# A hybrid trunk on one core: the tokens' rms as a scheduler stream of its own, and new VectorE prices in the scheduler

## Chip, cores and metric

The kernel runs on one core of a Trainium2 chip. The metric is the device time of one execution in microseconds (us). The profile comes from one execution of the same program.

## What is computed

Two layers on 528 tokens (16 meta tokens and 512 inputs) of width 1024, in float32. Cut to what matters here, one layer is:

```python
n = rms_norm(h, mix_norm_g)
q, k, v, qi, ki, wi, xr, yg, cv, gt = split(n @ w_in)
qi, ki = rotary(qi), rotary(ki)                 # indexer: 8 heads of 64
logits = einsum("bqhd,bsd->bqhs", qi, ki)
iscore = einsum("bqhs,bqh->bqs", relu(logits), wi * idx_scale)
sel = top_k(where(admissible, iscore, -inf), 128)   # 128 keys per query
attn = softmax attention of q over the chosen keys and values
rnn = gated linear recurrence of conv4(xr), times gelu(yg)
cnv = silu(layer_norm(conv31(glu(cv))))
merged = g_attn * (attn @ w_o_attn) + g_rnn * (rnn @ w_o_rnn) + g_conv * (cnv @ w_o_conv)
h = h + merged @ w_out
h = h + swiglu(rms_norm(h, ffn_norm_g))
```

## The kernel before

Activations are held with the channels on the partitions, in 8 tiles of 128 x 528. A float32 product is made of float32r parts: each weight tile of 128 x 1024 is loaded by SP's queue into a `raw` buffer, ScalarE copies its high part (`w<-raw`), and the low part is made either by ScalarE (negated copy) with an accumulating transfer on GpSimd's queue (`add_dma`, L401) or by VectorE. `gemm` then multiplies high weights with high and low inputs (L569) and low weights with high inputs (L579). PSUM is four pairs of banks.

Nothing in the program fixes an order by hand. Each job is a generator, a **stream**, that yields its operations one at a time; `Sched.run` simulates five engine clocks with prices and issues, step by step, the operation that can start first (among those within 40 ns of it on the same engine, the one of the best priority). The prices are the cost given with each operation, `LAT` (from the end of an operation to a reader on another engine) and `SELF` (to a reader on the same engine). They decide the order of the instructions on each engine; on the chip each engine then works through its own list in that order, and an instruction that waits holds up all behind it on that engine.

The streams that matter here:

- `main` (priority 40) runs the projection's tiles one after another: the keys of the indexer (`ki`), four tiles of its queries (`qi`), then `v_gemm`, which makes the values and the indexer's weights `wi` (L892), then K tiles, Conformer tiles, and so on. Its epilogues are streams of priority 10.
- The input's norm factor `r` (one number per token, spread over partitions) is made by `rsqrt2`: a sum on TensorE (L652), a root and a square on ScalarE, two operations on VectorE (L383). `r` scales the indexer's queries and keys.
- At the head of `v_gemm`, 4 small matmuls (L866) turn `r` so that tokens lie on the partitions, and VectorE writes `rtok` from them (L387). `v_epi` needs `rtok` to make `wi`. The matmuls on `r` write a half of a bank pair (`pr`), which is free again only when VectorE has read it; `v_gemm` goes on in halves like it, five at a time, and it is part of `main`, so its own matmuls are issued only after that read.
- `choose(i)` for i = 0 to 3 (priorities 36 to 39): 8 steps of scores (L954 or L963 on TensorE, relu on ScalarE, a multiply-add L383 on VectorE), then 16 rounds of `max` (L1004) and `match_replace` (L1005) on VectorE, over 144, 272, 400 and 528 keys. The masks are wanted by `heads` (L1235 on VectorE reads them).
- `k_epi` (rotation L380, then `rsqrt2` and a scaling L383), `ca_epi` and `conv` of the Conformer and recurrent branches share VectorE with it; `conv` is of the lowest priority.

Of the kernel before, what the change touches and what calls it, by code (L numbers as in the profile page):

```python
# [10 lines left out]
FR = mybir.dt.float32r  # L11
AF = mybir.ActivationFunctionType
ALU = mybir.AluOpType

L = 2
T = 528
# [9 lines left out]
TAKEN = -3.4e38  # L26
# [92 lines left out]
          "Abs_reciprocal_sqrt": ("a",)}  # L119
TABLE_LOAD = 1283.0  # L120
MOVE = {"SP": (310.0, 2000.0), "ACTQ": (310.0, 2000.0), "POOL": (210.0, 4300.0)}
SELF = {"PE": 0.0, "DVE": 125.0, "ACT": 110.0, "SP": 0.0, "POOL": 0.0}
LAT = {"PE": 170.0, "DVE": 100.0, "ACT": 130.0, "SP": 0.0, "ACTQ": 0.0, "POOL": 0.0}


class Sched:
    def __init__(self, make):
        self.make = make
        self.slots = {}
        self.clock = {e: 0.0 for e in LAT}  # L130
        self.table = None
# [50 lines left out]
    def spawn(self, gen, prio):  # L182
        self.n += 1
        s = [prio, self.n, gen, None]
        self.streams.append(s)
        self.step(s, None)
# [7 lines left out]
    def start(self, op):  # L194
        t = 0.0
        for b in op.R:
            assert b.live
            r = b.ready + (SELF[b.eng] if b.eng == op.eng else LAT[b.eng] if b.eng else 0.0)
            t = r if r > t else t
        for b in op.W:  # L200
            assert b.live
            if b.eng != op.eng:
                t = max(t, b.ready + (LAT[b.eng] if b.eng else 0.0))
            t = max(t, b.rd)
        return t, max(t, self.clock[op.eng])

    def run(self):
        while self.streams:
# [56 lines left out]
            for b in op.R:  # L265
                b.rd = max(b.rd, done + LAT[e])
            for b in op.W:
# [12 lines left out]
def trunk(ctx, tc, xT, wt, wv, wd, wg, gain_in, par_in, cst_in, id_in, out):  # L280
    nc = tc.nc
    V, S, PE = nc.vector, nc.scalar, nc.tensor

    const = ctx.enter_context(tc.tile_pool(name="const", bufs=1))
# [76 lines left out]
    free, spawn = sch.free, sch.spawn  # L361
# [28 lines left out]
    def dve(cost, fn, R, W):  # L390
        return Op("DVE", cost, fn, R, W)

    def pe(cost, fn, R, W):
        return Op("PE", 1.066 * cost, fn, R, W)
# [13 lines left out]
    def alloc(n=1, dt=FT, keep=0):  # L408
        return Alloc("s", n, dt, keep)
# [363 lines left out]
    def free_pairs(bs):  # L773
        for b in bs:
            free(*b.v)
# [4 lines left out]
    def layer(l, hs, h_src, h_next):  # L780
# [4 lines left out]
        HI, MID, LOW = P_HI, P_MID, P_CONV  # L785
# [68 lines left out]
        wib = boxes(4)  # L854
        rtok = Box()

        def v_gemm(w0, w1):
            vm = const.tile([128, 2, 256], FR, name="vmeta", bufs=1)
            vh = yield alloc(2, FR)
            vl = yield alloc(2, FR)  # L860
            r = yield rbox
            pr = yield Alloc("b1")

            def go():
                for i in range(4):
                    PE.matmul(pr[:, i:i + 1], r[:, NM + 128 * i:NM + 128 * i + 128], ones[:, 1, 0:1], start=True, stop=True)  # L866
            yield pe(900, go, [r], [pr])
            rt_ = const.tile([128, 4], FT, name="rtok", bufs=1)
            yield ts(rt_, pr[:, :4], -0.5 * IDX_SCALE, None, ALU.mult, None, [pr], [])
            free(pr)  # L870
            rtok.set(rt_)
            pss = [None] * 5
            for e, w in enumerate((w0, w1)):
                hi = yield w[0]
                lo = None
                for part in range(2):
                    if part:
                        lo = yield w[1]
                    for i in range(5):
                        t0, tn = (0, 128) if i == 0 else (NM + 128 * (i - 1), 128)  # L880
                        if not e and not part:
                            pss[i] = yield Alloc("b1")
                        ps = pss[i]
                        xk = []
                        for k in range(4 * e, 4 * e + 4):
                            xk.append((yield ns[k]))

                        def go(e=e, part=part, hi=hi, lo=lo, ps=ps, t0=t0, tn=tn, xk=xk):
                            for k, (nh, nl) in enumerate(xk):
                                o = 264 * k  # L890
                                for a, b in (((nh, hi), (nl, hi)), ((nh, lo),))[part]:
                                    PE.matmul(ps[:tn, :264], a[:, t0:t0 + tn], b[:, o:o + 264], start=e + part + k == 0 and a is nh,  # L892
                                              stop=bool(e and part and k == 3))
                        yield pe((920, 460)[part], go, [b for x in xk for b in x] + [(hi, lo)[part]], [ps])
                        if e and part:
                            if i == 0:
                                spawn(v_meta(ps, vm), HI)
                            else:
                                spawn(v_epi(i, tn, ps, vh[(i - 1) // 2], vl[(i - 1) // 2]), HI)
                    free((hi, lo)[part])  # L900
# [70 lines left out]
        def choose(i, box):  # L971
            w, o = W_OF[i], OFF[i]
            q0 = NM + 128 * i
            yield wib[i]
            if i in (0, 1, 3):
                sc = yield Alloc("u" if i == 0 else "s")
                box.set(sc)
            else:
                sc = yield box
            sv = sc[:, o:o + w]  # L980
            for hd in range(8):
                q = yield qi[hd // 2]
                k = yield ki
                t = q[hd % 2]
                ps, v, vw = yield from s_matmul(i, [(t[:, q0:q0 + 128], k[0]), (t[:, q0:q0 + 128], k[1 + hd % 2])], [t, *k], BC)
                rl = yield alloc()
                yield act(vw(rl[:, :w]), v, AF.Relu, [ps], [rl])
                free(ps)
                if hd == 0:
                    yield ts(sv, rl[:, :w], wi[i][:, 0:1], None, ALU.mult, None, [rl], [sc])  # L990
                else:
                    yield stt(sv, rl[:, :w], wi[i][:, hd:hd + 1], sv, ALU.mult, ALU.add, [rl, sc], [sc])
                free(rl)
            idx_left[0] -= 1
            if not idx_left[0]:
                free_pairs(qi)
                free(*ki.v)
                free(rbox.v)
                free(tabs[2].v, tabs[3].v)
            yield dve(80, lambda: V.memset(sv[:64, w - 64:], OUT_OF_REACH), [], [sc])  # L1000
            rows = slice(64, 128) if i == 0 else slice(0, 128)
            for _ in range(16):
                mx = const.tile([128, 8], FT, name=f"mx{i}", bufs=2)
                yield dve(70 + w / 0.96, lambda: V.max(mx[rows], sv[rows]), [sc], [])  # L1004
                yield dve(70 + w / 0.96, lambda: V.match_replace(sv[rows], mx[rows], sv[rows], TAKEN), [sc], [sc])  # L1005
            yield ts(sv[rows], sv[rows], -3e38, -BIG, ALU.is_gt, ALU.mult, [sc], [sc])
            if i == 0:
                yield dve(100, lambda: V.memset(sv[:64, :w - 64], 0.0), [], [sc])
                yield dve(80, lambda: V.memset(sv[:64, w - 64:], -BIG), [], [sc])
            masks[i].set(sc)  # L1010
# [88 lines left out]
        def rnn(c, u, a, m):  # L1099
            yield s4_in  # L1100
            tr = yield rt[0][c]
            sp, sn = s4p[:, l, c:c + 1], s4n[:, l, c:c + 1]
            yield act(a[:, :T], tr[:, :T], AF.Exp, [tr], [a], scale=sn, bias=sn)
            yield act(tr[:, :T], tr[:, :T], AF.Tanh, [tr], [tr], scale=sp, bias=sp)
            yield act(m[:, :T], a[:, :T], AF.Square, [a], [m])
            yield stt(m[:, :T], m[:, :T], 1.0, tr[:, :T], ALU.add, ALU.mult, [m, tr], [m])
            free(tr)
            ti = yield rt[1][c]
            yield stt(u[:, :T], ti[:, :T], 1.0, u[:, :T], ALU.add, ALU.mult, [ti, u], [u])
            free(ti)  # L1110
            yield act(m[:, :T], m[:, :T], AF.Sqrt, [m], [m], scale=0.25)
            yield tt(u[:, :T], u[:, :T], m[:, :T], ALU.mult, [u, m], [u])
            yield dve(620, lambda: V.tensor_tensor_scan(m[:, :T], a[:, :T], u[:, :T], 0.0, ALU.mult, ALU.add), [a, u], [m])
            free(a, u)
            gy = yield rg[c]
            yield tt(m[:, m0:T], m[:, m0:T], gy[:, m0:T], ALU.mult, [m, gy], [m])
            free(gy)
            x, y = yield alloc(2, FR)
            yield from split(x[:, m0:T], y[:, m0:T], m[:, m0:T], [m], x, y)
            free(m)  # L1120
            rs[c].set((x, y))
# [518 lines left out]
        mbox = boxes(4)  # L1640
        for i in range(4):
            spawn(choose(i, mbox[(0, 1, 0, 3)[i]]), P_CHOOSE + i)
        for c0 in range(2):
            spawn(conv(c0), LOW)
        for g in range(2):
# [123 lines left out]
```

## Time and profile before

| | |
|---|---|
| median of 3 executions | 2146.97 us (2145.22 to 2148.07) |
| the profiled execution | 2148.31 us, its span 2146.5 us |
| TensorE (PE) busy | 2093.8 us, 98% |
| its weight loads (PEld) | 1972.3 us, 92% |
| VectorE (DVE) busy | 1591.3 us, 74% |
| ScalarE (ACT) busy | 1361.0 us, 63% |
| GpSimd (POOL) busy | 318.8 us, 15% |
| the chain that ended last | PE 69%, DVE 10%, ACT 3% |

The span is the part of the execution that the profiler saw; the profiled execution is 1.3 us above the median. Busy times add up work of different stages, so a share over the span says little of a single stage: the stages have to be read one by one.

### The profile page before, as it was taken

The page shows a single profiled execution, that of the slowest core. Times are in us where ns is not written, and L with a number is a line of the kernel's source. Part 1 is how long each engine was busy: PE and PEld are TensorE (multiplying, and loading weights), DVE is VectorE, ACT ScalarE, POOL GpSimd, SP SyncE. Part 2 cuts the span into 40 slices and gives each one's busy share as a digit, 9 for nine tenths or more (in the row PEclk, how much of TensorE's full clock was granted, in tenths as well). Part 3 has the DMA queues.
Part 4 walks back from the last instruction along what each step waited for, and adds up shares of the span by engine and source line. Part 5 has one row for each costly group of instructions (what it writes and reads, how often), then busy time and mean ns, then how long its engine had stood idle before and what let it go on. Part 6 is the DMA issues. An engine that isn't in the chain of part 4 may idle for free.

```text
span 2146.5 us, 37980 instructions
## 1 busy us (share of the span) xinstructions
PE 2093.8 (98%) x14808; PEld 1972.3 (92%) x14808; DVE 1591.3 (74%) x2990; ACT 1361.0 (63%) x2114; POOL 318.8 (15%) x392
## 2 busy tenths in 40 slices
PE   7989999999999999999999899999999999999999
PEld 7989989999999999999999898988878888899997
DVE  7899958995337587677669999679962566777774
ACT  7657877876665565455457578888765646555552
POOL 1111101111111011111011121111111211111110
PEclk9999999999999999999999999999999999999999
DMA  8478546788897586657465675567889876766653
GB/s 232 106 171 187 133 91 125 174 179 173 177 214 175 131 194 162 139 138 162 114 195 138 165 181 133 122 135 168 184 181 190 195 180 161 182 153 143 159 137 108
DMA packets 127044, 342.67 MB, mean 160 GB/s; under 512 B 14864, under 2 KB 17040, under 8 KB 126864
## 3 DMA queue, kind: packets, MB, share of 16 engines
q0 software_dynamic: 50112, 145.47, 38.0%
q1 hardware_dynamic: 76608, 194.76, 30.9%
q8 instruction: 116, 1.90, 0.4%
q14 instruction: 64, 0.52, 0.1%
q10 hardware_dynamic: 144, 0.02, 0.0%
HBM read 327.91 MB, written 4.26 MB: 155 GB/s over the span
## 4 chain that ended last, share of the span: by engine, by line
PE 69%; DVE 10%; ACT 3%; issue 2%; DMA 1%; POOL 0%; SPq 0%; DVEq 0%; ACTq 0%; POOLq 0%
PE banks L569 31%; PE banks L579 15%; PE banks L610 12%; PE banks L614 6%; DVE s L383 3%; DVE s L380 3%; ACT s L377 2%; DVE mx L1004 1%; PE banks L1347 1%; DMA s<-in_wt_dram 1%; DVE s L1005 1%; PE banks L954 1%; PE banks L1087 1%; PE banks L1326 1%; DVE u L1005 1%
## 5 line engine op out<-in xcount | busy, mean ns | idle before, releaser
L569 PE MATMUL banks<-s,w 128*128 128x264 f32 (+1 forms) x6432 | 1033.4, 313 | 17.7 <-ACT w L377 7.3
L569 PEld LDWEIGHTS banks<-s,w 128*128 128x128 f32 x6432 | 906.5, 189 | 85.3 <-ACT w L377 7.3
L377 ACT ACTIVATE w<-raw 128x1024 fp32r<-128x1024 f32 (+3 forms) x486 | 479.0, 990 | 286.0 <-PE banks L569 137.5
L579 PE MATMUL banks<-s,w 128*128 128x264 f32 (+1 forms) x3216 | 543.6, 313 | 11.5 <-DMA w<-in_wt_dram 11.5
L579 PEld LDWEIGHTS banks<-s,w 128*128 128x128 f32 x3216 | 461.5, 190 | 47.7 <-DMA w<-in_wt_dram 13.1
L377 ACT ACTIVATE s<-s 128x512 fp32r<-128x512 f32 (+8 forms) x640 | 382.7, 615 | 175.4 <-DVE s L380 137.0
L380 DVE TENSOR_TENSOR s<-s,s 128x528 f32<-128x528 f32 (+8 forms) x522 | 331.0, 654 | 48.6 <-ACT s L377 41.0
L610 PE MATMUL banks<-s,s 128*128 128x264 f32 (+1 forms) x2464 | 347.3, 283 | 5.0 <-DVE s L380 2.5
L401 POOL DMA_DIRECT2D w<-in_wt_dram x192 | 167.3, 871 | 1183.6 <-ACT w L377 1011.7
L383 DVE SCALAR_TENSOR_TENSOR s<-s,half,s 128x512 f32<-128x512 f32 (+23 forms) x480 | 339.8, 743 | 2.8
L610 PEld LDWEIGHTS banks<-s,s 128*128 128x128 f32 x2464 | 318.5, 189 | 7.9 <-ACT s L377 3.1
L380 DVE TENSOR_TENSOR s<-s,banks 128x512 f32<-128x512 f32 (+3 forms) x340 | 195.5, 587 | 110.8 <-PE banks L614 67.6
L377 ACT ACTIVATE s<-banks 128x528 f32<-128x528 f32 (+11 forms) x338 | 165.0, 505 | 155.2 <-PE banks L614 75.4
L614 PE MATMUL banks<-s,s 128*128 128x264 f32 (+1 forms) x1232 | 198.5, 283 | 2.8 <-DMA s<-in_wt_dram 2.8
L401 POOL DMA_DIRECT2D s<-in_wt_dram x132 | 114.1, 864 | 517.8 <-ACT s L377 422.5
L377 ACT ACTIVATE s<-u 128x512 fp32r<-128x512 f32 x176 | 110.4, 627 | 102.3 <-DVE u L380 87.4
L614 PEld LDWEIGHTS banks<-s,s 128*128 128x128 f32 x1232 | 169.5, 189 | 3.2 <-DMA s<-in_wt_dram 3.2
L380 DVE TENSOR_TENSOR s<-u,s 128x512 fp32r<-128x512 f32 x176 | 119.7, 688 | 47.1 <-ACT s L377 42.9
L380 DVE TENSOR_TENSOR w<-raw,w 128x512 fp32r<-128x512 f32 (+2 forms) x94 | 76.1, 814 | 62.7 <-PE banks L569 40.8
L383 DVE SCALAR_TENSOR_TENSOR s<-s,banks 128x528 f32<-128x528 f32 (+1 forms) x48 | 33.2, 692 | 120.0 <-PE banks L579 114.9
L377 ACT ACT_TABLE_LOAD x80 | 102.6, 1283 | 4.9 <-DMA s<-in_xT_dram 3.7
L380 DVE TENSOR_TENSOR u<-s,s 128x512 f32<-128x512 f32 x88 | 60.3, 685 | 25.7 <-DMA s<-in_wt_dram 25.7
(129 smaller groups left out, 1273.5 us busy)
## 6 DMA issues: line engine op xcount, KB each, us to landing
raw<-in_wt_dram SPq DMA_DIRECT2D x206, 512.0 KB, 4.4
w<-in_wt_dram POOLq DMA_DIRECT2D x192, 512.0 KB, 7.7
s<-in_wt_dram SPq DMA_DIRECT2D x176, 256.0 KB, 5.1
s<-in_wt_dram POOLq DMA_DIRECT2D x132, 256.0 KB, 4.8
raw<-in_wd_dram SPq DMA_DIRECT2D x64, 256.0 KB, 2.9
raw<-in_wd_dram SPq DMA_DIRECT2D x16, 384.0 KB, 3.3
s<-s POOLq DMA_DIRECT2D x36, 132.0 KB, 5.6
s<-in_xT_dram SPq DMA_DIRECT2D x16, 264.0 KB, 4.6
```

Source lines behind the costliest of these rows:

```text
L377: return Op("ACT", cost, lambda: S.activation(o, i, f, **kw), R, W, TABLES.get(name))
L380: return Op("DVE", 69 + width(o) / 0.96, lambda: V.tensor_tensor(o, a, b, op), R, W)
L383: return Op("DVE", (69 if isinstance(s, float) else 129) + width(o) / 0.96, lambda: V.scalar_tensor_tensor(o, a, s, b, op0, op1), R, W)
L401: return Op("POOL", 1040.0, lambda: nc.gpsimd.dma_start(out=o, in_=i, accum_op=ALU.add), R, W, None, 4 * o.shape[0] * width(o))
L569: PE.matmul(o, hi[:, 128 * k:128 * k + 128], x, start=(k == ks[0] and i == 0), stop=False)
L579: PE.matmul(o, lo[:, 128 * k:128 * k + 128], x, start=False, stop=k == ks[nk - 1])
L610: PE.matmul(d, w[:, 128 * c:128 * c + 128], t[:, o:o + n], start=c == 0 and e == 0, stop=False)
L614: PE.matmul(d, w[:, 128 * c:128 * c + 128], h[:, o:o + n], start=False, stop=c == 3)
L954: PE.matmul(ps[:, :w], a, b[:, :w], start=e == 0, stop=e == n - 1)
L1004: yield dve(70 + w / 0.96, lambda: V.max(mx[rows], sv[rows]), [sc], [])
L1005: yield dve(70 + w / 0.96, lambda: V.match_replace(sv[rows], mx[rows], sv[rows], TAKEN), [sc], [sc])
L1087: PE.matmul(ps[:, h, :264], w[:, o:o + 128], b[:, 264 * h:264 * h + 264], start=i == 0, stop=i == 2)
```

## The change

Three things are changed, and no arithmetic.

1. `SELF` of VectorE goes from 125 to 15 ns; `LAT` of TensorE from 170 to 200, of VectorE from 100 to 125, of ScalarE from 130 to 140.
2. The prices of `max` and `match_replace` in `choose` go from 70 to 155 and 245 ns, each plus the width over 0.96; that of the scan in the recurrent branch from 620 to 1170 ns.
3. The making of `rtok` leaves `v_gemm` and becomes a stream `tokens`, spawned behind the four `choose` with the priority `HI`, which is 12.

```diff
-SELF = {"PE": 0.0, "DVE": 125.0, "ACT": 110.0, "SP": 0.0, "POOL": 0.0}
-LAT = {"PE": 170.0, "DVE": 100.0, "ACT": 130.0, "SP": 0.0, "ACTQ": 0.0, "POOL": 0.0}
+SELF = {"PE": 0.0, "DVE": 15.0, "ACT": 110.0, "SP": 0.0, "POOL": 0.0}
+LAT = {"PE": 200.0, "DVE": 125.0, "ACT": 140.0, "SP": 0.0, "ACTQ": 0.0, "POOL": 0.0}
...
-        def v_gemm(w0, w1):
-            vm = const.tile([128, 2, 256], FR, name="vmeta", bufs=1)
-            vh = yield alloc(2, FR)
-            vl = yield alloc(2, FR)
+        def tokens():
+
             r = yield rbox
             pr = yield Alloc("b1")
...
             rtok.set(rt_)
+
+        def v_gemm(w0, w1):
+            vm = const.tile([128, 2, 256], FR, name="vmeta", bufs=1)
+            vh = yield alloc(2, FR)
+            vl = yield alloc(2, FR)
...
-                yield dve(70 + w / 0.96, lambda: V.max(mx[rows], sv[rows]), [sc], [])
-                yield dve(70 + w / 0.96, lambda: V.match_replace(sv[rows], mx[rows], sv[rows], TAKEN), [sc], [sc])
+                yield dve(155 + w / 0.96, lambda: V.max(mx[rows], sv[rows]), [sc], [])
+                yield dve(245 + w / 0.96, lambda: V.match_replace(sv[rows], mx[rows], sv[rows], TAKEN), [sc], [sc])
...
-            yield dve(620, lambda: V.tensor_tensor_scan(m[:, :T], a[:, :T], u[:, :T], 0.0, ALU.mult, ALU.add), [a, u], [m])
+            yield dve(1170, lambda: V.tensor_tensor_scan(m[:, :T], a[:, :T], u[:, :T], 0.0, ALU.mult, ALU.add), [a, u], [m])
...
             spawn(choose(i, mbox[(0, 1, 0, 3)[i]]), P_CHOOSE + i)
+        spawn(tokens(), HI)
```

The instructions are the same in number on TensorE, VectorE, GpSimd and SP; ScalarE loads its function table once more. What changes is their order.

TensorE, first layer, from the second `qi` tile to the head of `v_gemm`; `w_236` and `w_303` are the high and low weights of that `qi` tile, `s_300` is `r`. Before:

```order
L569 MATMUL banks<-s_209,w_236 128x264 x2
L569 MATMUL banks<-s_210,w_236 128x264 x2
L579 MATMUL banks<-s_101,w_303 128x264 x2
...
L579 MATMUL banks<-s_209,w_384 128x264 x2
L866 MATMUL banks<-ones,s_300 128x1 x4
L892 MATMUL banks<-w_422,s_380 128x264
```

Now:

```order
L569 MATMUL banks<-s_209,w_236 128x264 x2
L569 MATMUL banks<-s_210,w_236 128x264 x2
L864 MATMUL banks<-ones,s_300 128x1 x4
L579 MATMUL banks<-s_101,w_303 128x264 x2
...
L579 MATMUL banks<-s_209,w_388 128x264 x2
L895 MATMUL banks<-w_424,s_379 128x264
```

The matmuls on `r` moved ahead of the low half of the second `qi` tile and of two whole tiles behind it.

VectorE at the same place; `s_300` is `r`, `s_95` the indexer's keys, `s_379` (now `s_378`) the first normed tile of `v_gemm`. Before:

```order
L383 SCALAR_TENSOR_TENSOR s_301<-banks,s_301 128x528
L337 TENSOR_TENSOR sp_y<-sp_z 128x16
L383 SCALAR_TENSOR_TENSOR s_300<-s_301,s_300 128x528
L338 TENSOR_SCALAR sp_p<-sp_y 128x16
...
L380 TENSOR_TENSOR s_318<-s_318,s_319 128x528
L387 TENSOR_SCALAR rtok<-banks 128x4
L340 SCALAR_TENSOR_TENSOR sp_p<-sp_p,sp_y 128x16
```

Now:

```order
L383 SCALAR_TENSOR_TENSOR s_301<-banks,s_301 128x528
L383 SCALAR_TENSOR_TENSOR s_300<-s_301,s_300 128x528
L383 SCALAR_TENSOR_TENSOR s_378<-s_93,neg,s_300 128x528
L383 SCALAR_TENSOR_TENSOR s_95<-s_95,s_300 128x528
L387 TENSOR_SCALAR rtok<-banks 128x4
L337 TENSOR_TENSOR sp_y<-sp_z 128x16
```

`rtok` moved from behind the rotation of two `qi` tiles to the third place behind `r`.

VectorE in the first layer's choices, around the norm of the first K tile (two L383 of `rsqrt2` that write its factor, a third that scales the tile); `u_784` (now `u_795`) are the scores of `choose(0)`, `s_796` (now `s_817`) those of `choose(1)`. Before:

```order
L1005 MATCH_REPLACE s_796<-mx_1255,s_796 128x272
L1004 MAX mx_1267<-u_784 64x8
L1004 MAX mx_1272<-s_796 128x8
L383 SCALAR_TENSOR_TENSOR s_1181<-banks,s_1181 128x528
L1005 MATCH_REPLACE u_784<-mx_1267,u_784 64x144
L383 SCALAR_TENSOR_TENSOR s_1180<-s_1181,s_1180 128x528
L387 TENSOR_SCALAR u_784<-u_784 64x144
L383 SCALAR_TENSOR_TENSOR s_775<-s_775,s_1180 128x528
```

Now:

```order
L1007 MAX mx_1191<-u_795 64x8
L1007 MAX mx_1184<-s_817 128x8
L383 SCALAR_TENSOR_TENSOR s_1118<-banks,s_1118 128x528
L383 SCALAR_TENSOR_TENSOR s_1117<-s_1118,s_1117 128x528
L383 SCALAR_TENSOR_TENSOR s_770<-s_770,s_1117 128x528
L1008 MATCH_REPLACE u_795<-mx_1191,u_795 64x144
L1007 MAX mx_1227<-u_795 64x8
```

The norm stood in the last round of `choose(0)`, at VectorE's row 184 of the program; it stands in the eighth round from the end now, at row 154, and its three steps follow one another.

## Rows read from the trace of the kernel before

**Rows 1.** The page's busy times: engine, us, share of the span, instructions.
```profile
PE 2093.8 (98%) x14808; PEld 1972.3 (92%) x14808; DVE 1591.3 (74%) x2990; ACT 1361.0 (63%) x2114; POOL 318.8 (15%) x392
```
**Rows 2.** Engine waits, TensorE: what ended them, us in total, times, longest.
```profile
PE banks L579 <- DMA w<-in_wt_dram: 11.5, 5, 3.3
PE banks L892 <- DVE rtok L387: 5.0, 1, 5.0
```
**Rows 3.** Busy us of each engine in chosen stretches, with TensorE's granted clock (PEclk).
```profile
core 0: us, PE busy (x) PEld busy (x) DVE busy (x) ACT busy (x) POOL busy (x), PEclk, DMA share, GB/s
107.30:161.00 53.70, 48.20 (x366) 47.64 (x365) 53.35 (x146) 29.22 (x36) 9.26 (x12) 0.94 0.75 171
28.75:32.16 3.41, 3.41 (x18) 3.41 (x17) 3.37 (x10) 1.99 (x4) 0.00 (x0) 0.50 0.90 197
49.23:56.06 6.83, 5.85 (x26) 5.85 (x27) 6.21 (x16) 2.57 (x4) 0.00 (x0) 0.50 0.47 111
110.67:114.08 3.41, 3.41 (x15) 3.41 (x16) 3.30 (x11) 1.27 (x3) 0.00 (x0) 0.50 0.65 167
137.98:141.39 3.41, 3.41 (x18) 3.41 (x17) 3.41 (x10) 0.14 (x1) 0.47 (x1) 0.50 1.02 240
1192.70:1196.10 3.40, 3.40 (x14) 3.11 (x13) 3.40 (x12) 1.06 (x1) 0.27 (x1) 0.50 1.05 274
```
**Rows 4.** Timeline of TensorE, 25 to 68 us: start, us, instruction, [idle before <-releaser].
```profile
25.73 0.41 PE L569 MATMUL banks<-s,w 128*128 128x264 f32 x2
28.01 3.31 PE L579 MATMUL banks<-s,w 128*128 128x264 f32 x16 [1.87 <-DMA w<-in_wt_dram]
...
43.22 0.95 PE L866 MATMUL banks<-ones,s 128*128 128x1 f32 x8
...
50.21 16.48 PE L892 MATMUL banks<-w,s 128*128 128x264 f32 x112 [4.97 <-DVE rtok L387]
```
**Rows 5.** Timeline of VectorE: `r` is written, and `rtok`.
```profile
29.70 0.71 DVE L383 SCALAR_TENSOR_TENSOR s<-s,s 128x528 f32<-128x528 f32 x1
...
50.00 0.15 DVE L387 TENSOR_SCALAR rtok<-banks 128x4 f32<-128x4 f32 x1
```
**Rows 6.** Timeline of TensorE: waits beside the choices, first layer and second.
```profile
110.66 5.71 PE L569 MATMUL banks<-s,w 128*128 128x264 f32 x32 [3.06 <-DVE s L383]
...
137.17 3.25 PE L579 MATMUL banks<-s,w 128*128 128x264 f32 x16 [2.44 <-DMA w<-in_wt_dram]
...
1146.30 0.52 PE L954 MATMUL banks<-s,s 128*128 128x272 f32 x2 [1.41 <-DVE wi L387]
...
1191.64 3.05 PE L579 MATMUL banks<-s,w 128*128 128x264 f32 x16 [2.66 <-DMA w<-in_wt_dram]
...
1214.92 2.20 PE L579 MATMUL banks<-s,w 128*128 128x264 f32 x16 [3.30 <-DMA w<-in_wt_dram]
```
**Rows 7.** Timeline of VectorE: the first K tile's norm factor.
```profile
109.91 0.69 DVE L383 SCALAR_TENSOR_TENSOR s<-banks,s 128x528 f32<-128x528 f32 x1
```
**Rows 8.** Timelines of ScalarE and GpSimd beside the same choices.
```profile
101.94 0.83 ACT L377 ACTIVATE s<-s,par,half 128x528 f32<-128x528 f32 x1 [5.64 <-DVE s L383]
...
112.81 0.65 ACT L377 ACTIVATE s<-s 128x528 fp32r<-128x528 f32 x1 [4.53 <-DVE s L383]
...
133.69 0.92 POOL L401 DMA_DIRECT2D w<-in_wt_dram  x1 [1.47 <-ACT w L377]
...
1201.77 0.82 ACT L377 ACTIVATE s<-s,par,half 128x512 f32<-128x512 f32 x1 [5.87 <-DVE s L383]
```
**Rows 9.** One source line: the choice's `match_replace`, durations min/median/max in ns.
```profile
L1005 DVE MATCH_REPLACE8 s<-mx,s x64: 411/560/696, 88.9 to 1248.2; 128x272 f32<-128x272 f32 x32, 128x528 f32<-128x528 f32 x32
```
**Rows 10.** Timeline of VectorE: `conv` steps of two channels in turn, and of one.
```profile
199.33 2.74 DVE L383 SCALAR_TENSOR_TENSOR s<-s,half,s 128x504 f32<-128x504 f32 x4
...
488.15 5.43 DVE L383 SCALAR_TENSOR_TENSOR s<-s,half,s 128x509 f32<-128x509 f32 x7
```
**Rows 11.** Timeline of VectorE: the last choice's mask, and the first head that reads one.
```profile
172.98 0.43 DVE L387 TENSOR_SCALAR s<-s 128x528 f32<-128x528 f32 x1
...
219.18 0.36 DVE L1235 CUSTOM_DVE_ANT_0 u<-banks,u,qr 128x144 f32<-128x144 f32 x1
```
**Rows 12.** Timeline of TensorE: a wait in the heads of the first layer.
```profile
292.83 0.56 PE L954 MATMUL banks<-s,s 128*128 128x144 f32 x3 [1.79 <-DVE qz L1181]
```

## The prediction, made before the change was run

> **What bounds the kernel now.** I read the page's busy times first: TensorE is busy for 2093.8 us, 98% of the span of 2146.5 us [rows 1]. A change of order removes no matmul, so all that it can win is TensorE's idle time, 2146.5 - 2093.8 = 52.7 us, and the stretches in which its clock was low. The waits of TensorE say what ended that idle time [rows 2]: low weights that land late (11.5 us in 5 waits) and one wait of 5.0 us for `rtok`. The busy times by stretch, with the granted clock, say where: VectorE is busy for 53.35 of 53.70 us in 107 to 161 us, where the choices run, while TensorE is busy for 48.20 [rows 3]. In that stage VectorE's order decides when TensorE may go on. The same view shows what a wait costs behind its end: TensorE is granted 0.50, the 1.2 GHz level, in the stretches that begin during or within a microsecond after the waits at 28, 50, 111, 137 and 1192 us, for 3.4 us each, and for 6.8 us in one case [rows 3]. Half of the busy time in such a stretch is lost: 1.7 us of 3.41, 2.9 of 5.85.
>
> Faster or slower means here by over 0.2%, 4.3 us, about what a measurement of this kernel can tell from no change.
>
> **Part 1, `rtok` alone.** TensorE stood 4.97 us for it until 50.21 [rows 4], since VectorE came to `rtok` only at 50.00 [rows 5]; the low clock behind it cost 2.9 us [rows 3]. `rtok` stands some 30 steps earlier on VectorE now, so both go: -7.9 us. But the matmuls on `r` move on TensorE's list too, ahead of the low half of the second `qi` tile, and everything behind them in that list waits with them. `r` is complete at 29.70 + 0.71 = 30.41 us [rows 5]; TensorE had ended its work at 25.73 + 0.41 = 26.14 and could go on at 28.01 [rows 4]. Now it waits until 30.4, does the 0.95 us of matmuls on `r`, and comes to that low half at 31.4: 3.4 us later, of which 0.95 is only moved from 43.22 [rows 4]. So 2.4 us are new; the low clock behind the old wait stays, and if the longer wait brings another such stretch it costs 1.7 more. Bounds 2.4 to 4.1; I take 3.0, nearer the lower end since the old wait already had its stretch. Part 1 is worth -7.9 + 3.0 = -4.9 us. In the second layer nothing waited for `rtok`, and `r` there is ready where the matmuls now stand: nothing.
>
> **Part 2, the choices' prices: first layer.** The wait of 3.06 us at 110.66 [rows 6] is for the first K tile's norm factor, whose first step VectorE began at 109.91 [rows 7], behind rounds of the choices. `match_replace` lasts 411 to 696 ns beside a load of its own [rows 9]; 70 + 272/0.96 = 353 and 70 + 528/0.96 = 620 ns were the old prices, so the scheduler believed VectorE further than it was. With the new ones it puts that norm 30 rows earlier (184 to 154 of VectorE's list), ahead of some 13 us of VectorE's work as the rows between them add up. It is then limited by its own input, not by the rounds; 3.06 + 1.7 of low clock [rows 3] go: -4.8. The wait at 137.17 is for a low weight, 2.44 us [rows 6]. It is late since GpSimd issued its transfer at 133.69, behind ScalarE's copy [rows 8], and ScalarE had stood 5.64 us at 101.94 and 4.53 us at 112.81 for VectorE's steps of the Conformer and K epilogues [rows 8]. Those steps move up by 8 to 14 us of VectorE's work: 2.44 + 1.7 = -4.1.
>
> **Part 2, second layer.** The same pattern: 1.41 us at 1146.30 for `wi` goes, as three K steps now stand ahead of that choice's scores (-1.4). The low weights at 1191.64 and 1214.92, 2.66 and 3.30 us [rows 6], come behind ScalarE's stand of 5.87 us at 1201.77 [rows 8] and others like it, and VectorE's steps that it waits for move up by 5 to 12 us: -(2.66 + 1.7) - 3.3 = -7.7. Parts 1 and 2 give -4.9 - 4.8 - 4.1 - 1.4 - 7.7 = -22.9 us.
>
> **What the new order costs.** With `SELF` at 15 ns the scheduler puts steps of one chain next to each other: over the whole program 729 neighbours on VectorE belong to one chain, 595 before, 134 more, most in the choices. On the chip that has a price: seven `conv` steps of one channel take 5.43/7 = 0.78 us each, four of two channels in turn 2.74/4 = 0.69 [rows 10]. At 0.09 us for each of 134 pairs VectorE works 12 us longer; at the other end, if short steps pay nothing, 0. The Trainium skill (VectorE: DVE Perf Modes, "The DRAIN you can't avoid") says that the next operation does not start until the pipe is empty and that chaining without semaphores changes nothing; by it neighbours cost the same in either order, and this part would be 0 us. The rows speak against that reading, by 0.09 us a step, and I count by them: 12 us of VectorE's work, some 4 us of it in each layer's choices. It is hidden at first: the last choice's mask was written at 172.98 and no head reads one before 219.18 [rows 11], 46 us of cover, of which the new order, which does the last score step of that choice late, uses some 15. If that cover were gone, each us would be one of TensorE's.
>
> The heads are the other place. In the first layer TensorE's transposes of one head stand 7 to 10 us earlier, while ScalarE's steps that feed them stand only 2 to 4 us earlier. A wait there was 1.79 us at 292.83 [rows 12]; that one goes, and I expect one or two new ones of 2 to 4 us with their low clock. Together +3. The waits in the feed-forward part keep their order and stay.
>
> Sum: -22.9 + 3 = -20 us from the profiled 2148.3, 2128.3; its median stood 1.3 lower, so **2127 us**.
>
> **The rivals.**
>
> *VectorE's chains come through.* 12 us of longer chains fall where VectorE is full (53.35 of 53.70 us [rows 3]) and push the epilogues that TensorE or ScalarE wait for: -20 + 12 = -8, 2139 us. For it speaks that most of the 134 pairs are in that stage, against it that the new order puts the epilogues before the rounds. Chance 0.15. By the skill's rule this could not be.
>
> *The waits only change their names.* VectorE has as much to do in the choices' stage as before; if ScalarE's and TensorE's waits for it come back at other steps, part 2 is worth nothing, and part 1 is left with its new wait at its upper bound, -7.9 + 4.1, plus a new wait of 2 us in the heads: 2145 us, no change. For it: prices alter the plan, not the chip, and the plan's waits were hidden from it before as well. Chance 0.12.
>
> *All small waits go too.* A plan nearer the chip also removes the small waits of 211 to 325 us and their low clock and their counterparts in the second layer, some 12 us: 2115 us. Chance 0.15.
>
> *Slower: the heads starve.* TensorE's list holds transposes and scores of each head ahead of where ScalarE's and VectorE's lists make their inputs; a wait like the 1.79 us of [rows 12] in each of the 16 head passes of both layers is 29 us, against the 23 won: +6, 2153 us. It decides from 13 passes on (13 x 1.79 = 23). Against it: only one head in the first layer and a few steps in the second show that lag in the order. Chance 0.08.
>
> **How the numbers follow.** The main case has 0.50. Main, chains and small waits end faster by over 4.3 us: 0.80; the third case the same: 0.12; starving heads slower: 0.08. The range reaches from the case of all small waits, 2114, to that of no change, 2145; slower cases, and a little at the lower end, are left out.
>
> **What would show it.** In the profile after, TensorE's waits hold no line for `rtok`; the matmuls on `r` stand before 31.5 us with a wait of some 4.3 us ended by VectorE's L383; the K tile behind 110 us starts without a wait and the granted clock stays at 1.00 there; the low weights at 137, 1192 and 1215 us are on time; VectorE's busy time grows by up to 12 us. Wrong it would be if TensorE's waits of a microsecond and more in 100 to 330 us and 1140 to 1420 us sum to as much as before, wherever they stand.

## The result, and the profile after

The changed kernel took 2119.2 us (median of 5, 2116.9 to 2127.1) where the kernel before took 2146.3: a ratio of 0.9875 with a 95% interval of 0.9862 to 0.9888, **27 us faster**. A second set of runs of the same kernel, among the experiments below, gave 0.9861 (0.9846 to 0.9875). The forecast was 2127.

The page of the changed kernel, the line that answers to [rows 1]:

```profile
PE 2086.1 (99%) x14808; PEld 1966.0 (93%) x14808; DVE 1598.8 (76%) x2990; ACT 1366.1 (65%) x2115; POOL 318.6 (15%) x392
```

TensorE is busy for 7.7 us less with the same 14808 instructions, since a matmul at the low clock counts as longer; the span fell from 2146.5 to 2117.4 us. The waits of TensorE, answering to [rows 2]:

```profile
PE banks L864 <- DVE s L383: 4.3, 1, 4.3
...
PE banks L957 <- DVE wi L387: 1.1, 1, 1.1
PE banks L579 <- DMA w<-in_wt_dram: 1.1, 1, 1.1
```

No line names `rtok` any more, and late low weights fell from 11.5 us in five waits to 1.1 in one (2.1 in two in a second execution of the same kernel). In their place stand a wait for `r` at its new place and a short one for `wi`. The timeline of TensorE over the stretch of [rows 4]:

```profile
23.74 2.38 PE L569 MATMUL banks<-s,w 128*128 128x264 f32 x18
30.41 1.87 PE L864 MATMUL banks<-ones,s 128*128 128x1 f32 x8 [4.29 <-DVE s L383]
32.14 3.48 PE L579 MATMUL banks<-s,w 128*128 128x264 f32 x16
...
47.11 14.75 PE L895 MATMUL banks<-w,s 128*128 128x264 f32 x120
...
66.14 0.89 PE L957 MATMUL banks<-s,s 128*128 128x272 f32 x4 [1.15 <-DVE wi L387]
```

`v_gemm` now runs in one piece. It ends at 61.86 us; before it ended at 50.21 + 16.48 = 66.69. Beside the choices, by stretch (answering to [rows 3]):

```profile
core 0: us, PE busy (x) PEld busy (x) DVE busy (x) ACT busy (x) POOL busy (x), PEclk, DMA share, GB/s
28.18:35.01 6.83, 4.60 (x21) 4.61 (x22) 5.75 (x15) 3.71 (x6) 0.87 (x1) 0.50 0.66 139
...
107.30:161.00 53.70, 53.70 (x441) 53.57 (x440) 51.27 (x135) 31.59 (x40) 11.29 (x15) 1.00 0.82 189
```

TensorE does not stop in 107 to 161 us and has its full clock (48.20 us busy at 0.94 before), and VectorE is no longer full (51.27 instead of 53.35). At the start the clock is low for 6.83 us, from within the wait for `r` on. The norm of the first K tile on VectorE, answering to [rows 7], and what waits around it:

```profile
94.56 0.45 DVE L1007 MAX8 mx<-s 128x8 f32<-128x272 f32 x1
94.92 0.69 DVE L383 SCALAR_TENSOR_TENSOR s<-banks,s 128x528 f32<-128x528 f32 x1
95.65 1.45 DVE L383 SCALAR_TENSOR_TENSOR s<-s,s 128x528 f32<-128x528 f32 x2
```

It begins at 94.92 instead of 109.91. ScalarE's longest stand for VectorE in 90 to 130 us, answering to [rows 8], is

```profile
112.74 0.83 ACT L377 ACTIVATE s<-s,par,half 128x528 f32<-128x528 f32 x1 [2.81 <-DVE s L383]
```

2.81 us where it had been 5.64 and 4.53.

To see where the time came from, I cut TensorE's work into stages by the work done, so that a stage holds the same amount of work in each kernel, and summed in each the start-to-start distances of neighbouring matmuls less the usual distance of their form in the kernel before. That is the time that TensorE lost to waits and low clock, worked out from the traces. Columns: the stage by us of work, the kernel before, the one changed, and six experiments told below; the last row also holds the little behind 1780.

```
work, us     before  after  choice_only  stream_only  old_choice  gate1  over_choice  over_far
   0-  70     14.7   11.3      15.0         10.7         12.5      11.0     12.5       12.6
  70- 160     10.3    0.7       1.1          8.3         10.8       1.1      0.7        0.8
 160- 330     12.5    7.4       7.1         19.5          8.6       7.4      9.4       26.2
 330-1125     11.6   13.4      12.5         11.3         11.1      10.8     11.9       22.5
1125-1250     12.3    4.3       2.6         17.6         17.0       3.4      0.6        0.6
1250-1450      5.8    5.1       5.6          3.8          1.7       5.6      2.3       30.2
1450-1690      6.9    5.3       7.4          6.6          6.6       5.6      4.6        9.8
1690-1780      3.6    0.4       0.9          3.4          0.4       3.4      0.4        3.1
all           77.5   48.4      52.6         81.4         69.0      48.6     43.0      106.0
```

29 us less is lost after the change, as much as the span fell. 9.6 of it lie in the first layer's choices (70 to 160), 8.0 in the second layer's (1125 to 1250), 3.3 in the first 70 us, 5.1 in the heads of the first layer (160 to 330), 3.2 in the feed-forward part (1690 to 1780).

A second execution of the changed kernel (`after_again` below), read in the same way, tells how steady this is: it lost 1.1 us more in the first 70 us of work, 1.9 less in 330 to 1125, and within 0.5 us of the same everywhere else. A difference of a microsecond between two kernels in the first stage, or of two in 330 to 1125, can therefore not be put down to their edits.

### The profile page after: what moved, and what is told of

It is laid out like the page before. It is cut to its first block, busy times and chain, and to the rows that moved or that the text cites. A ratio compares the mean times of both kernels' runs of the same rounds, so it can differ in the third digit from the quotient of the medians.

```text
span 2117.4 us, 38007 instructions
## 1 busy us (share of the span) xinstructions
PE 2086.1 (99%) x14808; PEld 1966.0 (93%) x14808; DVE 1598.8 (76%) x2990; ACT 1366.1 (65%) x2115; POOL 318.6 (15%) x392
## 5 line engine op out<-in xcount | busy, mean ns | idle before, releaser
L380 DVE TENSOR_TENSOR s<-s,s 128x528 f32<-128x528 f32 (+7 forms) x522 | 332.3, 655 | 49.6 <-ACT s L377 40.6
L383 DVE SCALAR_TENSOR_TENSOR s<-s,half,s 128x512 f32<-128x512 f32 (+22 forms) x480 | 341.5, 744 | 3.5 <-ACT s L377 0.5
L383 DVE SCALAR_TENSOR_TENSOR s<-s,banks 128x528 f32<-128x528 f32 (+1 forms) x48 | 33.2, 692 | 115.1 <-PE banks L579 114.9
```

Source lines behind the costliest of these rows:

```text
L380: return Op("DVE", 69 + width(o) / 0.96, lambda: V.tensor_tensor(o, a, b, op), R, W)
L383: return Op("DVE", (69 if isinstance(s, float) else 129) + width(o) / 0.96, lambda: V.scalar_tensor_tensor(o, a, s, b, op0, op1), R, W)
```

## The experiments

In the order of the questions: which part of the change made it, whether the prices' accuracy did, and whether `rtok` can be had cheaper. Each was timed in rounds beside the kernel before, and the ratio is to that.

**Prices alone** (`prices_only`): the kernel before with all new numbers, `rtok` left in `v_gemm`.

> All new prices, the making of rtok left at the head of v_gemm. Theory (the two parts add): the gain of 27 us less the 4.8 us by which v_gemm ended earlier (66.7 to 61.9 us), so about 2124 us; TensorE's wait of some 5 us for rtok is back, the waits of over 2 us at 110, 137, 1192 and 1215 us are not. Rival (the stream is what matters, the prices only reshuffle): 2138 us or more, with waits of over 2 us left in 100 to 330 us.

2123.1 us, ratio 0.9885 (0.9872 to 0.9899). As the theory had it; its wait for `rtok` is 5.72 us, the four waits beside the choices are gone. Its interval overlaps that of the changed kernel, so by the times alone the 4 us that the stream adds to the prices are not shown.

**The choices' prices alone** (`choice_only`):

```diff
-                yield dve(70 + w / 0.96, lambda: V.max(...
-                yield dve(70 + w / 0.96, lambda: V.match_replace(...
+                yield dve(155 + w / 0.96, lambda: V.max(...
+                yield dve(245 + w / 0.96, lambda: V.match_replace(...
```

> Only the prices of max and match_replace are new. Theory (these prices hid VectorE's true position from the scheduler): the waits at 110, 137, 1192 and 1215 us go, 2146.3 - 15, about 2131 us. Rival (SELF and LAT do it): those waits stay, 2143 us or more.

2124.0 us, ratio 0.9888 (0.9875 to 0.9902): as much as all prices together, and 7 us better than my theory had it. Two numbers make nearly the whole gain. `SELF`, `LAT` and the scan's price are worth nothing that these runs can tell. What is left of the waits read before, on TensorE:

```profile
PE banks L892 <- DVE rtok L387: 4.5, 1, 4.5
PE banks L579 <- DMA w<-in_wt_dram: 4.1, 4, 2.2
```

**The stream alone** (`stream_only`): `tokens` with all prices of before.

> The stream tokens, all prices as before. Theory: 2146.3 - 4.8, about 2141.5 us (2139 to 2144); no wait for rtok, a wait of 4.3 us for r, and the waits near 110 and 137 us still there. Rival (any new order loses the old waits): 2132 us or less.

A miss: 2152.7 us, ratio 1.0023 (1.0014 to 1.0033), slightly slower. The first 70 us lose 4.0 us less, as expected, but the order that the old prices then give loses 7 more in 160 to 330 and 5 more in 1125 to 1250. Its waits beside the choices are of the old kind, only longer:

```profile
120.28 4.11 PE L569 MATMUL banks<-s,w 128*128 128x264 f32 x17 [4.53 <-DVE s L383]
```

**The old choices' prices in the changed kernel** (`old_choice`): 70 for both again, all else new.

> The changed kernel with the old prices of max and match_replace alone. Theory (these prices make the gain, the rest rides on them): about 2145 us or more, with waits of over 2 us near 110 to 140 us and 1190 to 1220 us. Rival (SELF, LAT and the scan's price would do by themselves): 2130 us or less.

2141.4 us, ratio 0.9975 (0.9965 to 0.9985), a little under the bound that I set, and with what it named. The chain of [rows 8] is there to be followed, on ScalarE, GpSimd and TensorE:

```profile
122.17 0.83 ACT L377 ACTIVATE s<-s,par,half 128x528 f32<-128x528 f32 x1 [8.99 <-DVE s L383]
```
```profile
126.92 0.86 POOL L401 DMA_DIRECT2D w<-in_wt_dram  x1 [13.71 <-ACT w L377]
```
```profile
135.00 1.25 PE L579 MATMUL banks<-s,w 128*128 128x264 f32 x4 [7.11 <-DMA w<-in_wt_dram]
```

ScalarE stands 9 us for a VectorE step that is queued behind rounds of the choices; the weight copies behind it wait, GpSimd cannot issue a transfer for 13.7 us, and TensorE stands 7.1 us for the low weight. A wait put down to a transfer is VectorE's here.

**The choices' prices with the stream** (`choice_stream`): `SELF`, `LAT` and the scan as before.

> The choices' prices and the stream tokens, with SELF, LAT and the scan's price as before. Theory: 2124.0 of the choices' prices alone less 4.8 us for rtok, about 2119 us, the same as the changed kernel, so that SELF, LAT and the scan are worth nothing. Rival (they are needed once the stream moves VectorE's steps): 2124 us or more.

2124.8 us, ratio 0.9904 (0.9889 to 0.9918). A miss by 5 us: the stream wins 4.1 us in the first 70 us of work against `choice_only` and loses 4.5 in 1125 to 1250 by its order there, with one wait of

```profile
1283.77 2.57 PE L569 MATMUL banks<-s,w 128*128 128x264 f32 x10 [3.48 <-ACT s L377]
```

So the rest of the prices looks worth 6 us here (2119 against 2125) and nothing without the stream (2123.1 against 2124.0). Its interval begins where that of the changed kernel's first runs ends; whether it is those prices or the chance of one order among many, these runs do not settle.

**Prices too high** (`over_choice`): 240 and 420 instead of 155 and 245.

> The changed kernel with prices of max and match_replace too high: 240 and 420 ns plus the width over 0.96 where the trace has some 155 and 245. Theory (a price at the trace's value is what counts): waits come back, 2125 us or more. Rival (any higher price does it, since it only puts the choices' rounds behind the epilogues): 2120 us or less.

My theory fell: 2116.4 us, ratio 0.9856 (0.9843 to 0.987), no worse than with the trace's own durations, and its stage of 1125 to 1250 loses only 0.6 us. The first K tile's norm begins on VectorE at 94.88 us here, at 94.92 in the changed kernel and at 109.91 in the one before: a higher price does not move it further, since its own input comes no earlier. A price near the trace is not what counts.

**The same without the stream and the other prices** (`over_only`).

> The kernel before with only the choices' prices new, at 240 and 420 ns. Theory (order, not accuracy): as good as the choices' prices of the change alone (2124.0), 2120 to 2125 us. Rival (what over_choice won came from its joint order with SELF, LAT and the stream): 2128 us or more.

2126.2 us, ratio 0.9894 (0.9878 to 0.9909): a microsecond over the range that I gave, and within the interval of `choice_only`. Nor is accuracy needed there.

**Prices far too high** (`over_far`): 700 and 900. With the width added that is some 1.8 to 2.8 times what the steps last in the trace.

> The changed kernel with the choices' steps priced far too high, 700 and 900 ns plus the width over 0.96 (three times what they last). Theory (what counts is that the rounds stand behind the epilogues, and that the masks have cover before the heads): no waits of over 2 us in 70 to 160 us, but the choices end later on VectorE and the heads begin to wait; 2120 us or more. Rival (the more the better): 2116 us or less. Rival (a price near the trace is what counts): waits beside the choices are back, 2130 us or more.

2171.2 us, ratio 1.0103 (1.0085 to 1.0121). The stage of 70 to 160 loses 0.8 us in all, as the theory says, but the heads of both layers lose 26 and 30 us. The choices' `match_replace` in the changed kernel and then in this one (view of one line: durations min/median/max in ns, first and last start in us):

```profile
L1008 DVE MATCH_REPLACE8 s<-mx,s x64: 423/564/696, 85.3 to 1252.3; 128x272 f32<-128x272 f32 x32, 128x528 f32<-128x528 f32 x32
```
```profile
L1008 DVE MATCH_REPLACE8 s<-mx,s x64: 423/560/697, 87.6 to 1390.8; 128x272 f32<-128x272 f32 x32, 128x528 f32<-128x528 f32 x32
```

The rounds last the same, but the last of the second layer comes 138 us later, so late that the heads are held up (in the first layer their first step on the scores of 528 keys starts at 309.6 us instead of 227.1); in 1425 to 1470 us TensorE is busy for 33.78 of 45.00 us:

```profile
1425.00:1470.00 45.00, 33.78 (x185) 28.30 (x185) 43.99 (x114) 36.62 (x89) 0.00 (x0) 0.85 0.07 14
```

**The matmuls on `r` later** (`gate1`):

```diff
+        tok_on = Box()
+
         def tokens():
             r = yield rbox
+            yield tok_on
...
-        kinds = {"I": lambda k: [go(B_QI + k, ...)],
+        kinds = {"I": lambda k: [go(B_QI + k, ...)] + ([lambda: mark(tok_on)] if k == 1 else []),
```

> The changed kernel, with tokens let go only when the second qi tile has been issued, so that the matmuls on r stand behind that tile's low half. Theory: TensorE waits 1.9 us for the low weight instead of 4.3 us for r, and the low clock lasts 3.4 instead of 6.8 us: 2.4 to 4.1 us off, 2115 to 2117 us where the changed kernel has 2119.2. Rival (the matmuls' place costs nothing net, or the rest of the order pays it back): 2119 us or more.

2120.5 us, ratio 0.9873 (0.9859 to 0.9886): no gain. Its waits, on TensorE, and the stretch behind the last of them:

```profile
27.65 2.23 PE L579 MATMUL banks<-s,w 128*128 128x264 f32 x16 [1.66 <-DMA w<-in_wt_dram]
30.27 1.05 PE L866 MATMUL banks<-ones,s 128*128 128x1 f32 x8 [0.39 <-DVE s L383]
...
64.13 0.88 PE L959 MATMUL banks<-s,s 128*128 128x272 f32 x4 [3.08 <-DVE wi L387]
```
```profile
65.10:68.50 3.40, 3.40 (x17) 3.39 (x16) 2.08 (x6) 1.97 (x5) 0.00 (x0) 0.50 0.00 0
```

The wait for `r` shrinks from 4.29 to 0.39 us, and `v_gemm` begins at 42.91 instead of 47.11. But the scores need `wi`, which VectorE makes only when it is through the indexer's queries: that wait grows from 1.15 to 3.08 us and brings a low clock of 3.4 us, 1.7 us lost. Of 4.2 us, 2.0 arrive at the scores and 0.3 are left behind the low clock. The second execution of the changed kernel comes to the same scores 1.25 us later than the first (67.39 us), so what is left is no more than two executions of one kernel differ by here. Later in the program `gate1` is 2.5 us ahead of the changed kernel once more, and loses it in the feed-forward part, where a wait of 2.05 us is back; the next section says what it stands for.

**The recurrence's constants out of `r`'s way** (`derived_gate`): `gate1`, and the stream of the `sp_` tiles waits until the values are made.

> gate1, and the constants of the recurrence (sp_ tiles: 16 small VectorE steps, an exponential and its table load on ScalarE) held back until the values are made. They stood in front of r: ScalarE's table load of 1.28 and exponential of 0.22 us lie between the root and the square that r needs. Theory: r is ready 1.4 us earlier, VectorE is through the indexer's queries 3 us earlier, the wait of 3.1 us for wi and its low clock shrink: 2114 to 2117 us. Rival (VectorE does the same steps a little later, beside the choices, where it is full): 2119 us or more.

2119.3 us, ratio 0.9871 (0.9858 to 0.9885): again no gain. Nothing waits for `r` now, but `wi` comes 0.6 us earlier, not 3, and 0.6 is less than two executions of one kernel differ by there. The wait for it, and VectorE's idle times ahead of it in 50 to 63 us:

```profile
63.54 0.89 PE L961 MATMUL banks<-s,s 128*128 128x272 f32 x4 [2.96 <-DVE wi L389]
```
```profile
54.11 0.70 DVE L382 TENSOR_TENSOR s<-s,s 64x528 fp32r<-64x528 f32 x1 [1.08 <-ACT s L379]
55.73 2.80 DVE L382 TENSOR_TENSOR s<-s,s 64x528 fp32r<-64x528 f32 x4 [0.92 <-ACT s L379]
...
62.93 0.42 DVE L382 TENSOR_TENSOR s<-banks,s 128x256 fp32r<-128x256 f32 x1 [0.88 <-ACT s L379]
```

VectorE has less to do ahead of `wi` and now stands for ScalarE's halves of the same splits: the third engine in a row that sets this time.

**Both, with prices too high** (`over_gate`).

> derived_gate with the prices 240 and 420: the later place of the matmuls on r, the recurrence's constants out of r's way, and the choices' rounds behind the epilogues. Theory (the parts lie in different stages and add): 2116.4 less the 1.5 us by which gate1's first 70 us are shorter than over_choice's, 2113 to 2116 us. Rival (the new order pays it back): 2118 us or more.

2118.0 us, ratio 0.9862 (0.9843 to 0.9881). It loses least in the first 70 us (9.4), and gives it back in the first layer's heads (13.0 against 9.4). The changed kernel beside it (`after_again`):

> The changed kernel once more, beside the next three: 2119 us, to see whether the too-high prices are truly ahead of it (2116.4 in another session).

2118.8 us. The changed kernel, `over_choice`, `over_gate`, `gate1` and `derived_gate` cannot be told apart: none beats the change.

## Why the prediction was right, and where it was off

The direction and the mechanism held; the gain was 27 us where 20 were forecast. The sign that I had named for being wrong did not come: TensorE's waits of a microsecond and more fell from 9.1 us in four to none in 100 to 330 us, and from 8.6 us in four to 1.3 in one in 1140 to 1420 us. By stage, parts 1 and 2 measured 3.3 + 9.6 + 8.0 = 20.9 us where I had 22.9. The rest of the gain, in the heads and the feed-forward part, no step of the prediction forecast; that the total beat the forecast is luck.

- **`rtok`.** Forecast: -7.9, with 3.0 new, -4.9. `v_gemm` ended 4.83 us earlier. The wait for `r` was forecast to end at 30.4 (30.41 in the trace, 31.28 in the second execution) and the low half behind it to start at 31.4; it started at 32.14, since the low clock held the matmuls on `r` too (1.87 us for 0.95) and lasted 6.83 us, the bound that I had called less likely. What I missed is the next wait: 1.15 us for `wi`, so that 3.3 us are left over the first 70 us of work. The wait on `rtok` stood in front of VectorE's own path through the indexer's queries; removing it uncovers that path, as `gate1` shows in full. I also took the two parts to add. With the old prices (`stream_only`) and beside the choices' prices alone (`choice_stream`) the stream saves its 4 us in the first stage as well, but the order that comes with it loses as much or more elsewhere.
- **The choices, first layer.** Forecast -4.8 and -4.1; the stage 70 to 160 lost 9.6 us less. Right in size, and `choice_only` shows that the two choices' prices do it; `old_choice` shows the chain from VectorE over ScalarE and GpSimd to the late weight. One row I read wrongly: the transfer that TensorE waited for at 137.17 is not the one issued at 133.69 but the one before it, issued at 129.06, 8.1 us ahead; the one of 133.69 had still to land when that wait ended. ScalarE's stand in front of it was a later and shorter one than the two that I named. On ScalarE and GpSimd, before:

```profile
124.30 0.83 ACT L377 ACTIVATE s<-s,par,half 128x528 f32<-128x528 f32 x1 [3.09 <-DVE s L383]
```
```profile
129.06 0.86 POOL L401 DMA_DIRECT2D w<-in_wt_dram  x1 [8.91 <-ACT w L377]
```

The chain is the one that I described, and the forecast did not hang on which stand it was.

- **The choices, second layer.** Forecast -1.4 and -7.7; the stage 1125 to 1250 lost 8.0 less. Here, too, one row was put to the wrong wait: ScalarE's stand at 1201.77 cannot have delayed the weight that TensorE had at 1191.64. Its transfer was issued at 1184.03, behind a stand of 4.14 us for VectorE at 1178.81.
- **Why the prices do it.** I said that the scheduler believed VectorE further than it was. That is true of the old prices and not the reason: too high a price does as well (`over_choice`). What counts is the order that follows, the epilogues' steps ahead of the choices' rounds, as long as the rounds end before the heads ask for the masks. `over_far` lies past the end of that cover. The order was changed only by way of prices; setting it directly, with the old prices, was not tried.
- **The heads, the step that failed.** I added 3 us for new waits there. The stage of 160 to 330 lost 5.1 us less and that of 1250 to 1450 0.7 less. I had seen TensorE's transposes move up by more than what feeds them, and took the lag for a wait. No such wait came: beside the 1.79 us that I expected to go, one of 1.84 us at 311 us went too, and in 100 to 330 us none of a microsecond is left. Why the lag costs nothing I have not worked out.
- **The feed-forward part** I held to be unchanged. It lost 3.2 us less in 1690 to 1780. `gate1` and `derived_gate` lose 3.4 and 3.5 there, the kernel before 3.6, the changed one and `old_choice` 0.4, without an edit in that part. The traces tell what goes with it. In the chain that ended last of the kernel before, a transfer of weights into one of the `s` buffers stands there:

```profile
1817.67 12.32 DMA s<-in_wt_dram
```

VectorE stood 2.22 us for it, and TensorE 2.50 us for VectorE 12 us later. VectorE stands 1.3 to 3.0 us for that transfer in each of the five traces that lose 3 us and more in this stage (the kernel before, `stream_only`, `gate1`, `derived_gate`, `over_far`), and in none of the other nine but `choice_stream`, where it stands 0.56 us and the stage loses 1.5. It is not the order: from 1120 us on, TensorE, VectorE, ScalarE and GpSimd work through the same steps in the same order in `gate1` and in the changed kernel, as far as the traces name them. `gate1` comes there 2.5 us ahead and is 0.4 us behind after it. Why the transfer lands in time in some kernels and not in others stays open.

- **VectorE's longer chains.** Forecast up to 12 us of its work, hidden. Busy time grew by 7.5 us (1591.3 to 1598.8). `choice_only` has 1589.4 and `prices_only` 1597.9, so the growth comes with `SELF`, `LAT` and the scan's price, and their times are 2124.0 and 2123.1: hidden indeed, and the rival of 2139 us did not come. The single steps add up to nearly the same, 1743.6 us before and 1745.2 after; what shrank is their overlap. Of VectorE's 2990 steps 1965 began before the one ahead had ended, and 1880 do so now, 85 fewer (I had counted on 134 pairs). The prediction took the Trainium skill (VectorE: DVE Perf Modes, "The DRAIN you can't avoid") to mean that neighbours cost the same in any order. The 7 to 8.5 us more for the same 2990 instructions do not agree with that reading. That section also says that a next operation that is not held starts earlier, and with this the 1880 early starts agree. Neighbours by themselves were not tried.
- **The rivals.** "All small waits go too" (2115) lies 4 us below the result, and part of it happened: of the waits of over 1.2 us in 290 to 330 us none is left. The result stands nearer to this rival than to the main case, though not by its mechanism alone: part of the difference is the feed-forward part. "The waits only change their names" is what `stream_only` did, without new prices. "The heads starve" is what `over_far` did, by another way (the masks came late) and at a price that the change is far from.

## What to carry to other kernels

In a list-scheduled kernel, price the long, patient chain of an engine rather high than low: too low, and more of its steps are laid ahead of the short ones that other engines wait for than the chip gets through in time. Here prices 85 and 175 ns too high cost nothing that the runs can tell, and prices of 700 and 900 ns, with which the chain's own reader had to wait, cost 52 us. Follow a wait for a weight back over the queues before blaming the transfer; it ended here at VectorE, two engines away. And before paying for an earlier result, look for the next thing its reader needs: 4 us won at `v_gemm` became 0.3 behind the scores, less than two executions of one kernel differ by.

## What the runs showed of the hardware

A wait can cost more than its length. Around the 4.29 us of waiting for `r`, from 28.18 us on, TensorE was granted 0.50 (1.2 GHz) for 6.83 us; behind 3.08 us in `gate1` for 3.4 us. Others cost no low clock at all: in `prices_only` the waits of 0.51, 0.74 and 1.14 us before 42 us (the granted clock is 1.00 from 20 to 45 us), and in `gate1` the wait of 1.66 us that ends at 27.65, where the kernel before had waited 1.87 us and was granted 0.50 for 3.41 us [rows 3].

On VectorE the next step often starts before the one ahead has ended, but not always. In the rows of the changed kernel above, the first step of the norm starts 0.09 us before the `MAX8` of 272 keys ends (94.56 + 0.45 = 95.01), and both use all 128 partitions. A step that reads what the one ahead wrote starts after its end: the second step of that norm 0.04 us after the first (94.92 + 0.69 = 95.61). In the choices' rounds that alternate between 64 and 128 partitions the next step starts 0.03 us after the end as well:

```profile
99.61 0.31 DVE L1007 MAX8 mx<-u 64x8 f32<-64x144 f32 x1
99.95 0.45 DVE L1007 MAX8 mx<-s 128x8 f32<-128x272 f32 x1
```

These two depend on nothing of each other, and the cause is not `MAX8` itself: in the changed kernel all 12 `MAX8` on 128 partitions that follow one on 64 start 0.01 to 0.03 us after its end, and all 11 that follow another choice's `MAX8` on 128 partitions start 0.08 us before it. The Trainium skill (VectorE: DVE Perf Modes, "Two Vector instructions with no wait between them") gives a model in which an instruction whose operands start in another group of 32 partitions than those ahead starts only when all earlier ones are finished. `choose(0)` works on partitions 64 to 127, the others on 0 to 127, and the rows agree. Interleaving those two choices saves VectorE nothing.
